# The gated sum of two branches, turned by transposing transfers in place of TensorE, in a decoder block on one Trainium2 core

## The chip, the cores and the metric

One NeuronCore of one Trainium2 chip runs the kernel. It has five engines that run beside each other, each with its own queue of instructions: TensorE (PE, matmuls; its weight loads are listed as PEld), VectorE (DVE), ScalarE (ACT), GpSimd (POOL) and SyncE (SP), which in this kernel mostly issues DMAs. The metric is the device time of one execution in microseconds (us); lower is better.

## What is computed

A decoder block over 256 positions of width 2048, in float32. The part that matters here:

```python
proj = a @ w_in[layer]                       # a = rmsnorm(h, ...)
q_a, k_a, v_a, q_r, f_r, i_r, g_r, gate_a, gate_r = split_columns(proj)
...
y = jax.nn.sigmoid(gate_a) * (attn @ w_attn_branch[layer]) + jax.nn.sigmoid(gate_r) * (r_out @ w_hgrn_branch[layer])
h = h + rmsnorm(y @ w_mix_out[layer], norm_mix_post[layer])
a = rmsnorm(h, norm_ffn_pre[layer])
gt, up = jnp.split(a @ w_ffn_gate_up[layer], [D_FF], axis=-1)
ff = (jax.nn.silu(gt) * up) @ w_ffn_down[layer]
h = h + rmsnorm(ff, norm_ffn_post[layer])
```

`attn` is a dilated sliding-window attention, `r_out` a gated linear recurrence; `y` is 256 x 2048, `w_mix_out` 2048 x 2048. To multiply `y` by `w_mix_out`, the contracted dimension, y's columns, must lie on the 128 partitions: y has to be transposed in between.

## The kernel before

**Matmuls.** Every weight and every activation is split into a high part (fp32r, ScalarE) and a low part (what is missing, VectorE), and a product is three matmuls: high by high, high by low, low by high. Weights come in by DMA into one of three `raw` slots, are split into one of three `w` slots, and are read by TensorE. A loop at the end of `tile_hybrid_block` goes over a list of items. For item i it first calls `prepare(i)`, which splits the weights of item i+2 and issues the load that is three `raw` slots further on, then issues the matmuls of item i, and then resumes, one step each, the generators that hold the rest of the work: `evacs` (reading out finished accumulators), `turned`, `turns` (two resumptions per item, L1663), and the `lanes`. A generator does the work up to its next `yield` and is resumed later; a deque of them is worked from the front, and `flush` runs it to the end. The order in which instructions are issued here is the order on each engine.

**Two kinds of items stand around the change.** The branches' weights are multiplied in blocks of 512 columns ("N" blocks), four chunks each, 12 matmuls of 128 x 512 per chunk. The four blocks of `w_attn_branch` are called B0 to B3 here, and B2c1 is chunk 1 of block B2. Two chunks share one `raw` slot. Then come the two wide blocks of `w_mix_out`, of eight steps each; the steps of the first are called s0 to s7. Six of them, (m, 0) in `MIX[0]`, have 24 matmuls and read slot m of `yT`; s3 and s6, (0, 1) and (1, 1), are done with seven products for eight, 21 matmuls, and read sums of slots 0 and 1 (`y7`, made by `pair_sums` in a lane). By the list the slots are read in this order: s0 reads slot 2, s1 slot 3, s2 slot 4, s3 slot 0, s4 slot 5, s5 slot 6, s6 slot 1, s7 slot 7.

**Accumulators.** There are four banks `acc` and four `aux`. A block B takes two of `acc`, a step s0 takes the banks (0, 0) and (0, 1) for the first half of its matmuls and (1, 0), (1, 1) for the second; the last two are those of B3, free once `evac_attn_branch(3)` has read them (L1174).

**The gated sum.** `evac_attn_branch(j)` is resumed in the three items after block j's last chunk. The first two multiply the accumulators by the gate and add the other branch's part (L1174, L1175), so that y_j, 256 x 512, lies in the gate's own tile; the third appends the generator `turned` of y_j to `turns`. Here that is called round j; it makes slots 2j and 2j+1 of `yT`. For each slot it issues four transposes of 128 x 128 on TensorE into an `aux` bank (L598), yields, then calls `put`: high part on ScalarE (L575), low part on VectorE (L579), and yields. What a step reads comes through `after(turns)`: where the slot isn't there yet, the generators in `turns` are resumed on the spot until it is, so that the step's own matmuls are issued behind them.

Before the first mix step `begin_mix` runs `evacs` to the end, loads an activation table and issues six DMAs from ScalarE's queue (L1186 to L1196). After step s1 `turns` is flushed (L1602).

**The feed-forward part** turns its own activations in another way, in `turn_act` (L1366): ScalarE splits the 32-bit words into a plane of low and a plane of high 16-bit halves (L1370), SP issues four transposing transfers of 16-bit elements (L1376), and ScalarE joins the two planes again (L1385).

Of the kernel before, what the change touches and what calls it, by code (L numbers as in the profile page):

```python
# [14 lines left out]
F32 = mybir.dt.float32  # L15
F32R = mybir.dt.float32r
I32 = mybir.dt.int32
U16 = mybir.dt.uint16
AF = mybir.ActivationFunctionType
OP = mybir.AluOpType  # L20

P = 128
S = 256
# [78 lines left out]
def tile_hybrid_block(ctx: ExitStack, tc: tile.TileContext, t, out):  # L102
    nc = tc.nc
# [12 lines left out]
    def nm(s):  # L116
        serial[0] += 1
        return f"{s}_{serial[0]}"
# [7 lines left out]
    def aux():  # L126
        return auxp.tile([P, 512], F32, tag="aux", name=nm("aux"))
# [4 lines left out]
    def p3(s, dtype, n, bufs, tag=None):  # L132
        return wide_pool[-1].tile([P, n], dtype, tag=tag or s, bufs=bufs, name=nm(s))
# [33 lines left out]
    ident = cpool.tile([P, P], F32, name="ident")  # L167
# [50 lines left out]
    blocks, chunks, wides, steps = [], [], [], []  # L218
# [27 lines left out]
    def add_wide_block(*args, **kw):  # L246
        b = Wide(*args, **kw)
        wides.append(b)
        for i in range(len(b.order)):
            n = len(steps)  # L250
            slots.append(lambda n=n: load_wide(n))
            items.append((steps, n, len(slots) - 1))
            steps.append([b, i, None, None])
# [296 lines left out]
            yield  # L550


    class Split:


# [31 lines left out]
                return self(k)  # L587
            return x

        def turned(self, src, n0, n):  # L590

            for i in range(n):
                ps = aux()
                for kk in range(2):
                    for b in range(2):
                        at = kk * S + b * P
                        c = (2 * i + kk) * P
                        nc.tensor.transpose(ps[:, at : at + P], src[:, b, c : c + P], ident)  # L598
                yield
                self.put(n0 + i, ps.rearrange("p (k t) -> p k t", k=2))  # L600
                yield

    def transpose_in(src, gcol, dst, c, apart=False):
# [43 lines left out]

    evacs, turns, lanes, queue = deque(), deque(), [deque(), deque()], deque()
    back, turned, hold = deque(), deque(), [False]
    ready = set()  # L650

    def advance(q):
        if q:
            try:
                next(q[0])
            except StopIteration:
                q.popleft()
                return

    def flush(q):  # L660
        while q:
            advance(q)
# [494 lines left out]
    yT = []  # L1157
# [10 lines left out]
    def evac_attn_branch(j):  # L1168
        def go(banks):
            if not yT:  # L1170
                yT.append(Split("yT", KD))
            y = gates["a", j]
            for i in range(2):
                nc.vector.tensor_mul(y[:, i, :], banks[i], y[:, i, :])  # L1174
                nc.vector.tensor_add(y[:, i, :], y[:, i, :], part[j][:, i, :])  # L1175
                yield
            turns.append(yT[0].turned(y, 2 * j, 2))
        return go


# [396 lines left out]
    for half in range(2):  # L1577
        for g in range(3):
            c = 1024 * g + 512 * half
# [16 lines left out]
    for j in range(2):  # L1596
        last_mix = len(wides)
        add_wide_block(t["w_mix_out"][0], (1024 * j, 1024 * j + 512), MIX[j],
                       lambda k: yT[0].after(turns)(k), lambda m: y7[m], evac_mix, j == 0,
                       pre=begin_mix if j == 0 else None)  # L1600
        if j == 0:
            wides[-1].post = lambda c: flush(turns) if c == 1 else None  # L1602
    together = len(items) - 2
    w = t["w_ffn_gate_up"][0]
    spare = None
# [28 lines left out]
    for i in range(len(items)):  # L1634
        kind, n, _ = items[i]
        b, c = kind[n][:2]
# [22 lines left out]
        if wide and c == b.turn:  # L1659
            flush(evacs)  # L1660
            turned.append(turn_act(turns.popleft()))
        advance(turned)
        for _ in range(2):  # L1663
            if turns and type(turns[0]) is not tuple:
# [71 lines left out]
```

## Time and profile before

| | |
|---|---|
| median of 3 runs | 1688.17 us (1687.39 to 1688.42) |
| the profiled execution | 1689.89 us |
| its span, first to last instruction | 1688.1 us |
| granted TensorE clock, mean | 0.999 |
| DMA, mean | 248 GB/s |
| ScalarE, busy | 983.1 us, 1102 instructions |
| VectorE, busy | 1416.6 us, 1623 instructions |

The profile is of one execution. Its times count from the span's start: the attention branch's blocks B1 to B3 and the steps s0 to s5 lie between 865 and 938 us. In a timeline a row gives start, duration, engine, line of the kernel, operation, `out<-in` by the kernel's names, the shape and the count of instructions that were merged; in brackets stands how long the engine was idle before and what ended it. `PEld`, `SPq` and `ACTq` are the weight loads and the queues of SyncE and ScalarE. Rows of one source line give the smallest, median and largest duration in ns, and then the start of the first and the last one.

### The profile page before, as it was taken

The page shows a single profiled execution, that of the slowest core. Times are in us where ns is not written, and L with a number is a line of the kernel's source. Part 1 is how long each engine was busy: PE and PEld are TensorE (multiplying, and loading weights), DVE is VectorE, ACT ScalarE, POOL GpSimd, SP SyncE. Part 2 cuts the span into 40 slices and gives each one's busy share as a digit, 9 for nine tenths or more (in the row PEclk, how much of TensorE's full clock was granted, in tenths as well). Part 3 has the DMA queues.
Part 4 walks back from the last instruction along what each step waited for, and adds up shares of the span by engine and source line. Part 5 has one row for each costly group of instructions (what it writes and reads, how often), then busy time and mean ns, then how long its engine had stood idle before and what let it go on. Part 6 is the DMA issues. An engine that isn't in the chain of part 4 may idle for free.

```text
span 1688.1 us, 21672 instructions
## 1 busy us (share of the span) xinstructions
PE 1674.2 (99%) x8169; PEld 1406.0 (83%) x8169; DVE 1416.6 (84%) x1623; ACT 983.1 (58%) x1102; POOL 3.9 (0%) x13
## 2 busy tenths in 40 slices
PE   9999999999999999999999999999999999999997
PEld 7888888888888888888888888888888888888886
DVE  6899888867987987776668888898888988898987
ACT  6655555544455545555535547676667666675653
POOL 0000000000000000000000000000000000000000
PEclk9999999999999999999999999999999999999999
DMA  8566666668777866787858556898888888887673
GB/s 278 207 232 242 224 226 227 234 231 298 233 251 250 281 226 225 254 307 264 309 175 274 194 183 209 272 282 270 272 266 283 271 274 266 277 280 267 236 256 128
DMA packets 252841, 419.26 MB, mean 248 GB/s; under 512 B 36752, under 2 KB 103488, under 8 KB 250176
## 3 DMA queue, kind: packets, MB, share of 16 engines
q1 hardware_dynamic: 242480, 379.70, 68.1%
q10 hardware_dynamic: 10192, 38.15, 5.9%
q8 instruction: 64, 1.05, 0.3%
q14 instruction: 41, 0.34, 0.1%
q0 software_dynamic: 64, 0.02, 0.0%
HBM read 376.92 MB, written 35.13 MB: 244 GB/s over the span
## 4 chain that ended last, share of the span: by engine, by line
PE 95%; DVE 2%; ACT 1%; DMA 1%; issue 1%; SPq 0%; DVEq 0%; ACTq 0%
PE acc L139 62%; PE aux L139 32%; DVE wl L421 1%; PE aux L944 0%; DMA raw<-in_w_ffn_gate_up 0%; ACT w L419 0%; DMA x<-in_x 0%; PE aux L611 0%; DVE fz L1509 0%; DVE dl L431 0%; ACT junk L1463 0%; PE aux L598 0%; DVE e L1459 0%; DVE wl L428 0%; DVE f L543 0%
## 5 line engine op out<-in xcount | busy, mean ns | idle before, releaser
L139 PE MATMUL acc<-xT,w 128*128 128x256 f32 (+1 forms) x2048 | 365.1, 338 | 0.0
L421 DVE TENSOR_TENSOR wl<-raw,w 128x2048 fp32r<-128x2048 f32 (+1 forms) x140 | 304.5, 2182 | 67.3 <-ACT w L419 65.3
L139 PEld LDWEIGHTS acc<-xT,w 128*128 128x128 f32 x2048 | 311.9, 188 | 44.7
L366 DVE TENSOR_TENSOR w<-raw,w 128x1024 fp32r<-128x1024 f32 x176 | 215.0, 1222 | 118.9 <-ACT w L365 118.3
L419 ACT ACTIVATE w<-raw 128x2048 fp32r<-128x2048 f32 (+1 forms) x140 | 254.5, 1826 | 97.4 <-PE acc L139 31.6
L365 ACT ACTIVATE w<-raw 128x1024 fp32r<-128x1024 f32 x176 | 185.9, 1058 | 192.8 <-PE acc L139 137.4
L139 PE MATMUL acc<-w,xT 128*128 128x512 f32 x578 | 168.8, 391 | 0.0
L440 ACT ACTIVATE w<-sum 128x1024 fp32r<-128x1024 f32 x57 | 60.6, 1062 | 168.5 <-DVE sum L435 161.7
L139 PE MATMUL acc<-w,hT 128*128 128x512 f32 x472 | 152.7, 391 | 0.4 <-DVE hT L1259 0.4
L448 DVE TENSOR_TENSOR wl<-sum,w 128x1024 fp32r<-128x1024 f32 x114 | 137.2, 1221 | 7.7 <-ACT w L440 7.6
L139 PEld LDWEIGHTS acc<-w,xT 128*128 128x128 f32 x578 | 108.2, 188 | 22.3
L139 PE MATMUL aux<-w,hT 128*128 128x512 f32 x374 | 120.0, 389 | 0.0
L139 PE MATMUL aux<-w,xT 128*128 128x512 f32 x344 | 109.8, 389 | 0.0
L450 DVE TENSOR_TENSOR dl<-raw,dh 128x1536 fp32r<-128x1536 f32 x57 | 100.1, 1757 | 11.3 <-ACT dh L446 8.2
L139 PEld LDWEIGHTS acc<-w,hT 128*128 128x128 f32 x472 | 88.5, 188 | 19.0 <-DVE hT L1259 0.9
L139 PE MATMUL acc<-wl,hT 128*128 128x512 f32 x236 | 91.8, 389 | 0.0
L446 ACT ACTIVATE dh<-raw 128x1536 fp32r<-128x1536 f32 x57 | 84.1, 1475 | 5.3 <-PE acc L139 3.1
L139 PE MATMUL acc<-w,a 128*128 128x512 f32 x268 | 83.7, 389 | 0.2 <-DVE e L1413 0.2
L139 PEld LDWEIGHTS aux<-w,hT 128*128 128x128 f32 x374 | 70.2, 188 | 14.5
L139 PE MATMUL acc<-w,so 128*128 128x512 f32 x240 | 80.4, 389 | 0.0
L139 PE MATMUL aux<-w,a 128*128 128x512 f32 x254 | 79.5, 389 | 0.0
L139 PEld LDWEIGHTS aux<-w,xT 128*128 128x128 f32 x344 | 64.6, 188 | 13.4
(295 smaller groups left out, 2990.2 us busy)
## 6 DMA issues: line engine op xcount, KB each, us to landing
raw<-in_w_in SPq DMA_DIRECT2D x270, 512.0 KB, 4.7
raw<-in_w_ffn_gate_up SPq DMA_DIRECT2D x156, 512.0 KB, 5.0
raw<-in_w_ffn_down SPq DMA_DIRECT2D x88, 512.0 KB, 5.4
pre<-in_w_ffn_gate_up SPq DMA_DIRECT2D x40, 512.0 KB, 6.5
presum<-pre ACTq DMA_DIRECT2D x20, 1024.0 KB, 4.7
s<-presum SPq DMA_DIRECT2D x40, 512.0 KB, 6.9
raw<-in_w_mix_out SPq DMA_DIRECT2D x32, 512.0 KB, 5.0
act<-acts SPq DMA_DIRECT2D x22, 512.0 KB, 6.2
```

What stands on the lines that cost most here:

```text
L139: nc.tensor.matmul(ps, lhsT, rhs, start=start, stop=stop, skip_group_check=True)
L365: nc.scalar.activation(wh, raw, AF.Copy)
L366: nc.vector.tensor_sub(wl, raw, wh.bitcast(F32))
L419: nc.scalar.activation(hi[:, c], raw[:, c], AF.Copy)
L421: nc.vector.tensor_sub(lo[:, c], raw[:, c], hi[:, c].bitcast(F32))
L440: nc.scalar.activation(hi[:, :1024], s[:, :1024], AF.Copy)
L446: nc.scalar.activation(dhi, d, AF.Copy)
L448: nc.vector.tensor_sub(lo[:, c], s[:, c], hi[:, c].bitcast(F32))
L450: nc.vector.tensor_sub(dlo, d, dhi.bitcast(F32))
```

## The change

`Split.turned` no longer uses TensorE. A round now takes a second tile `flat` of 128 x 1024 words (tag "so", four buffers) and does this:

- ScalarE splits each half of y_j into two planes of 16-bit halves in `flat` (two instructions, `halves_apart`);
- SP issues four transposing transfers of 128 x 512 16-bit elements each, from `flat` into the tile of y_j, seen as two planes;
- six yields;
- ScalarE joins both planes into 32-bit words in `flat` (one instruction, `halves_joined`), and a yield;
- `put` of the two slots as before, now from `flat`, a yield after each.

The flush of `turns` moves from after s1 to after s4.

```diff
+    def halves_apart(flat, words):
+        nc.scalar.activation(
+            flat.bitcast(U16).rearrange("p (z c) -> p z c", z=2),
+            words.bitcast(U16).rearrange("p (c z) -> p z c", z=2), AF.Copy,
+        )
+    def halves_joined(words, planes):
+        nc.scalar.activation(
+            words.bitcast(U16).rearrange("p (c z) -> p z c", z=2), planes, AF.Copy
+        )
...
-        def turned(self, src, n0, n):
-            for i in range(n):
-                ps = aux()
-                for kk in range(2):
-                    for b in range(2):
-                        at = kk * S + b * P
-                        c = (2 * i + kk) * P
-                        nc.tensor.transpose(ps[:, at : at + P], src[:, b, c : c + P], ident)
+        def turned(self, src, spent, n0):
+            for b in range(2):
+                halves_apart(spent[:, b, :], src[:, b, :])
+            planes = src.rearrange("p b c -> p (b c)").bitcast(U16).rearrange(
+                "p (z k t) -> p z k t", z=2, k=4
+            )
+            for b in range(2):
+                for z in range(2):
+                    nc.sync.dma_start_transpose(
+                        planes[:, z, :, b * P : (b + 1) * P],
+                        spent[:, b, :].bitcast(U16)[:, z * 512 : (z + 1) * 512],
+                    )
+            for _ in range(6):
                 yield
-                self.put(n0 + i, ps.rearrange("p (k t) -> p k t", k=2))
+            words = spent.rearrange("p b c -> p (b c)")
+            halves_joined(words, planes.rearrange("p z k t -> p z (k t)"))
+            yield
+            for i in range(2):
+                self.put(n0 + i, words[:, i * 512 : (i + 1) * 512].rearrange("p (k t) -> p k t", k=2))
                 yield
...
-            turns.append(yT[0].turned(y, 2 * j, 2))
+            flat = p3("flat", F32, 1024, 4, "so").rearrange("p (b c) -> p b c", b=2)
+            turns.append(yT[0].turned(y, flat, 2 * j))
...
-            wides[-1].post = lambda c: flush(turns) if c == 1 else None
+            wides[-1].post = lambda c: flush(turns) if c == 4 else None
```

## The prediction

> **What bounds the kernel now.** I read the page's first part and its chain first, then the timeline of PE around the mix.
>
> ```profile
> PE 1674.2 (99%) x8169; PEld 1406.0 (83%) x8169; DVE 1416.6 (84%) x1623; ACT 983.1 (58%) x1102; POOL 3.9 (0%) x13
> PE 95%; DVE 2%; ACT 1%; DMA 1%; issue 1%; SPq 0%; DVEq 0%; ACTq 0%
> ```
>
> PE is busy for 99% of the span and 95% of the chain that ends last runs over it. So time leaves the kernel when PE gets less to do, and comes in whenever PE waits; what ACT, DVE or the DMAs get to do is free only as long as PE does not wait for it. The timeline of PE, from chunk B3c0 to mix step s4:
>
> ```profile
> 892.14 8.46 PE L139 MATMUL acc<-w,attnT 128*128 128x512 f32 x36
> ...
> 900.43 0.60 PE L598 MATMUL aux<-ident,gate 128*128 128x128 f32 x4
> 900.79 2.99 PE L139 MATMUL acc<-w,attnT 128*128 128x512 f32 x12
> 903.62 0.60 PE L598 MATMUL aux<-ident,gate 128*128 128x128 f32 x4
> 903.97 0.48 PE L139 MATMUL acc<-w,yT 128*128 128x512 f32 x1
> ...
> 907.19 0.50 PE L139 MATMUL acc<-w,yT 128*128 128x512 f32 x1 [0.21 <-DVE gate L1174]
> ...
> 910.05 0.60 PE L598 MATMUL aux<-ident,gate 128*128 128x128 f32 x4
> 910.40 0.48 PE L139 MATMUL acc<-w,yT 128*128 128x512 f32 x1
> ...
> 915.95 0.60 PE L598 MATMUL aux<-ident,gate 128*128 128x128 f32 x4
> 916.30 0.48 PE L139 MATMUL acc<-w,yT 128*128 128x512 f32 x1
> ...
> 921.88 0.39 PE L139 MATMUL aux<-w,so 128*128 128x512 f32 x1
> ...
> 926.64 0.39 PE L139 MATMUL acc<-w,yT 128*128 128x512 f32 x1
> ```
>
> Columns are start, duration, instruction and, in brackets, idle time. From 921.88 to 926.64 are the 21 matmuls of s3: 0.227 us each, so a chunk of 12 takes 2.72 and a step of 24 takes 5.45. Four transposes hold PE from 900.43 to 900.79, 0.36 us, and the 12 matmuls behind them take 2.83 up to 903.62, 0.11 more than 2.72. A group of four costs about 0.46 us. The transposes stand where nothing waits: PE has no idle time in these rows but 0.21 us at 907.19, for an accumulator bank that DVE's gate product frees.
>
> **What the change takes away.**
>
> ```profile
> L598 PE MATMUL aux<-ident,gate x32: 270/272/273, 876.8 to 916.3; 128*128 128x128 f32 x32
> L575 ACT ACTIVATE yT<-aux x8: 577/598/600, 877.4 to 918.2; 128x512 fp32r<-128x512 f32 x8
> L579 DVE TENSOR_TENSOR yT<-aux,yT x8: 680/688/693, 878.0 to 920.1; 128x512 fp32r<-128x512 f32 x8
> L575 ACT ACTIVATE a<-act x44: 609/614/632, 1436.0 to 1660.1; 128x512 fp32r<-128x512 f32 x44
> L579 DVE TENSOR_TENSOR a<-act,a x44: 680/684/695, 1438.4 to 1664.5; 128x512 fp32r<-128x512 f32 x44
> ```
>
> 32 transposes in 8 groups at 0.46 us are 3.7 us of PE. The puts stay, and their source moves from PSUM to SBUF: 0.60 and 0.69 us from aux, 0.61 and 0.68 from SBUF in the other rows, so nothing.
>
> **What it adds.** The same four operations already run in the feed-forward part (L1370 to L1385), so they have rows:
>
> ```profile
> L1370 ACT ACTIVATE e<-e x20: 1037/1042/1060, 1089.7 to 1468.8; 128x1024 uint16<-128x1024 uint16 x20
> L1385 ACT ACTIVATE act<-e x20: 1337/1374/1385, 1101.5 to 1482.2; 128x1024 uint16<-128x1024 uint16 x20
> 1093.47 6.33 SPq L1376 DMA_TRANSPOSE e<-e  x4
> 1101.52 2.61 ACT L1385 ACTIVATE act<-e 128x1024 uint16<-128x1024 uint16 x2 [0.74 <-DMA e<-e]
> L1376 SPq DMA_TRANSPOSE e<-e x4: 1337/1890/2399, 1418.5 to 1424.1; - x4
> DMA to landing us min/median/max: 4.3/6.8/8.3
> raw<-in_w_mix_out SPq DMA_DIRECT2D x32, 512.0 KB, 5.0
> ```
>
> A round gets two splits into planes at 1.04 us (ACT), four transposing transfers, and one join. The join takes both planes at once, 2048 halves; no row shows that. A pair of 1024 each took 2.61 us (1101.52), one alone 1.37; I take 2.6; 1.4, the lower end, would take 4 x 1.2 = 4.8 us off the sum. The transfers were issued from 1093.47, and the ACT instruction that needs them all could start at 1101.52: 8.0 us. In the other window the last was issued at 1424.1 and landed 4.3 later, 9.9 us after the first issue at 1418.5. A plain 512 KB load lands in 5.0, the lower end. I take 8.0. Each round is thus a serial chain of 2.1 + 8.0 + 2.6 + 0.6 = 13.3 us ahead of the first matmul that reads it, and 0.7 more ahead of the third, which reads the low part. In before, that was 0.36 + 0.6.
>
> By the Trainium skill (Advanced Engine Details and Errata, X-Bar Transpose) a transposing DMA is as fast as a regular one. The rows here do not agree for four small ones issued one behind the other; by that rule the first rival below would hold.
>
> **Where these chains lie.** The generator is resumed twice per chunk or step. It starts the transfers in its 1st resumption, joins in the 7th, puts in the 8th and 9th and ends in the 10th, and rounds queue behind each other. y_0 is evacuated by B1c2, so round 0 has resumptions 1 and 2 after B1c2, 3 and 4 after B1c3, 5 and 6 after B2c0, joins after B2c1 and ends after B2c2. In the same way round 1 starts after B2c3, joins after B3c2; round 2 starts only after s0, and s2 itself, which reads slot 4, pulls its join; round 3 starts after s3, is flushed after s4, and s5 reads slot 6. In the trace ACT, DVE and SP keep the program's order, so I follow their queues in the trace's own times. What I need:
>
> ```profile
> 874.23 1.06 ACT L365 ACTIVATE w<-raw 128x1024 fp32r<-128x1024 f32 x1 [1.65 <-PE acc L139]
> 880.22 0.88 SPq L270 DMA_DIRECT2D raw<-in_w_attn_branch  x2
> 896.72 0.28 DVE L523 SCALAR_TENSOR_TENSOR s<-f 128x128 f32<-128x128 f32 x1
> 897.65 1.22 DVE L366 TENSOR_TENSOR w<-raw,w 128x1024 fp32r<-128x1024 f32 x1
> 903.65 2.28 DVE L421 TENSOR_TENSOR wl<-raw,w 128x2048 fp32r<-128x2048 f32 x1
> 904.25 0.60 ACT L575 ACTIVATE yT<-aux 128x512 fp32r<-128x512 f32 x1 [0.78 <-PE aux L598]
> 904.87 1.28 ACT L1186 ACT_TABLE_LOAD   x1
> 906.46 0.68 DVE L1174 TENSOR_TENSOR gate<-acc,gate 128x512 f32<-128x512 f32 x1
> 908.52 1.92 ACT L419 ACTIVATE w<-raw 128x2048 fp32r<-128x2048 f32 x1 [2.37 <-DVE gate L1174]
> 918.68 1.92 ACT L419 ACTIVATE w<-raw 128x2048 fp32r<-128x2048 f32 x1
> SPq L288 <- DMA raw<-in_w_mix_out: 8.8, 2, 7.1
> ```
>
> A chunk's high part takes 1.06 on ACT and its low part 1.22 on DVE, a mix step's 1.92 and 2.28. Each waits for the weight slot of three items before, so it starts when PE ends that item, and PE reads it two items later.
>
> *Round 0.* Splits behind the 874.23 row: 875.3 to 877.4. SP's next load waits for the low part of B2c1, now at 879.7, and ends at 880.6. Transfers 880.6 to 888.6, join 891.2, put 891.8. Behind the join on ACT stands the high part of B3c0: 892.9, low part 894.1. PE, four groups earlier, is there at 892.14 - 1.8 = 890.3. It ends B3c0 at 894.1 + 11 x 0.227 = 896.6 and not 893.0: **3.6 lost**.
>
> *Round 1.* High part of B3c1 894.6, splits 896.7; SP's load, behind the low part of B3c1, ends at 897.5; transfers until 905.5, join 908.1, put of slot 2 908.7, low 909.4. PE is through B3c3 at 904.8 and waits for slot 2 until 908.7: 3.9. Behind the put: high part of s1 910.6, its low part on DVE 912.9, low of slot 3 913.6, the four small sums 1.0 (896.72 to 897.65) 914.6, and only then the gate product (0.68) that frees the bank of s0's second half, 915.3, where before it ended at 907.14. The first half ends at 909.4 + 10 x 0.227 = 911.7, so PE waits another 3.6. s0 ends at 918.0; before at 910.05: **8.0 behind**, all transposes so far credited.
>
> *Round 2.* ACT behind the last put (911.2): table load and six DMA issues, 904.85 to 908.52 before, so 914.9; high part of s2 916.8; splits 918.9. SP: the load of s5 waits for the first half of s4's load to land (7.1 us of SP waiting in the last row; 8.1 from that load's issue behind the low part of s1), 921.1, ends 922.0. Transfers until 930.0, join 932.6, put of slot 4 933.2, low 933.9. s1 ends at 918.0 + 5.5 = 923.5: PE waits 9.7. s2 ends at 933.9 + 22 x 0.227 = 938.9; before 921.88: **17.0 behind**.
>
> *Round 3.* High part of s5 waits for the end of s2: 941.0; splits 943.1; low part 943.3, SP's load 944.2, transfers 952.2, join 954.8, put 955.4, low 956.1. s4 ends at 938.9 + 4.8 + 5.4 = 949.1: PE waits 6.3. s5 ends at 956.1 + 5.0 = 961.1; before at 926.64 + 2 x 5.45 = 937.5: **23.6 behind**. Nothing gives that back, since PE is the bound of what follows. The rest of the added ACT work (19 us in all) and the loads that stand behind transfers on SP cost nothing: ACT is idle 42% of the span, and the tightest load, that of s4, lands at 921.0 for a split at 923.5. Without that cover a late load would hold PE by its lateness.
>
> **The clock.** PE has no gap like these in before except at the ends:
>
> ```profile
> 1.19 3.31 PE L139 MATMUL aux<-warm 128*128 128x512 bf16 x8 [1.19 <-DVE warm L163]
> 1678.18 0.39 PE L139 MATMUL aux<-w,a 128*128 128x512 f32 x1
> 1680.00:1688.10 8.10, 0.00 (x0) 0.00 (x0) 3.55 (x9) 0.65 (x4) 0.00 (x0) 0.71 0.39 129
> ```
>
> After the last matmul (1678.57) the granted clock averages 0.71 from 1680.0: a fall to half at about 1683.4, 4.8 us after PE stopped. The first eight matmuls took 3.31 us, 1.5 more than 8 x 0.227. So I price each gap over 4.8 us, those of 9.7 and 6.3, at 1.5 us: 3.0. Bounds: 0 and, with the gaps of s0, 6.
>
> By the Trainium skill (TensorE: Matmul & The Clock Gate, Part 1) an idle window of about 3.4 us halves the clock and 3.4 us of work restores it; by that, as an estimate, one of the gaps of s0 could cost 1.7 as well.
>
> **Sum.** 23.6 + 3.0 = 26.6 us, with the 3.7 saved in it. The profiled execution took 1689.9 (span 1688.1); with the change 1716.5. The median of the runs is 1.7 lower: 1688.2 + 26.6 = **1714.8 us**.
>
> **Rivals.**
> *The transfers cost what a plain load costs.* With 5.0 for 8.0 every chain is 3.0 shorter, and the four add up where each round starts later for the one before: 23.6 - 12 = 11.6, and one gap (6.7 at s2) still trips the clock: 13.1, **1701.3 us**. For it: the 5.0 row. Against: the four are issued one by one, some 1.3 to 2.4 us each, and both windows above took longer. This is what the Trainium skill's rule on X-Bar Transpose would give.
> *Not slower: all is hidden.* Then 3.7 of PE and the 0.2 at 907.19 go: **1684.3 us**. Its place is s2. Between the end of the high part of s2 (910.44) and the end of s1 (916.30) there are 5.9 us in before; the splits, join and put take 5.3 of them. It holds if the four transfers land within 0.6 us, or if round 2 starts a block earlier than I count.
> *Worse.* With 9.9 for 8.0 four chains give 7.6 more and a third gap trips the clock: 23.6 + 7.6 + 4.5 = 35.7, **1723.9 us**. For it: the second window took that long. Against: the first took 8.0.
> *The change does not do what it says* (TensorE keeps its transposes): 1688.2.
>
> **How the numbers follow.** Forecast 0.68, plain-load price 0.15, worse 0.09, hidden 0.05, no change 0.03. The range reaches from the first rival to the worse one: 1701 to 1724; below it lie the last two, 0.08, and some of each end. A measurement of this kernel tells 0.2%, 3.4 us, from no change. Faster 0.05, same 0.03, slower 0.92.
>
> **What would show it.** In the profile after: no L598 on PE; ACT's joins waiting for transposing transfers, four times, the longest in s1 to s2; PE idle ahead of B3c0, twice in s0 (ended by a put of yT, then by the gate product), about 10 us ahead of s2 and 6 ahead of s5; a granted clock under 1.00 behind these two; the same pace everywhere else. I am wrong if the joins start without waiting, if PE's wait at s2 is short, or if the stretch from B1c2 to s5 is under 10 us longer.

## The result and the profile after

| | before | after |
|---|---|---|
| median of 4 runs each | 1687.88 us (1687.39 to 1688.42) | 1713.53 us (1711.58 to 1713.74) |
| the profiled execution | 1689.89 us | 1713.74 us |
| its span | 1688.1 us | 1711.8 us |
| granted TensorE clock, mean | 0.999 | 0.992 |

The ratio is 1.0148 [1.0135, 1.0160]: the changed kernel is about 25 us slower, 23.7 us between the two profiled spans. The predicted time was 1714.8 us, with a range of 1701 to 1724. That is close, but two errors of opposite sign lie under it, and what its rivals said of a quicker landing was wrong.

The first part of the page and the first line of the chain, of after:

```profile
PE 1679.1 (98%) x8137; PEld 1407.5 (82%) x8137; DVE 1416.9 (83%) x1623; ACT 1000.4 (58%) x1114; POOL 3.8 (0%) x13
PE 88%; DVE 4%; DMA 3%; ACT 2%; issue 1%; SPq 1%; ACTq 0%; DVEq 0%
```

PE has 32 instructions fewer (8169 to 8137) and yet more busy time (1674.2 to 1679.1): some matmuls ran slower. ACT has 12 instructions and 17.3 us more. The chain lost 7% of PE to waits on DVE, DMA and ACT. The timeline of PE in after shows which:

```profile
889.85 0.50 PE L139 MATMUL acc<-w,attnT 128*128 128x512 f32 x1 [0.91 <-ACT w L365]
891.11 10.99 PE L139 MATMUL acc<-w,attnT 128*128 128x512 f32 x47 [0.76 <-DVE w L366]
904.74 0.50 PE L139 MATMUL acc<-w,yT 128*128 128x512 f32 x1 [2.64 <-ACT yT L588]
...
911.00 0.79 PE L139 MATMUL acc<-w,yT 128*128 128x512 f32 x1 [2.94 <-DVE gate L1196]
...
914.02 0.39 PE L139 MATMUL acc<-wl,yT 128*128 128x512 f32 x1
...
920.39 0.39 PE L139 MATMUL acc<-w,yT 128*128 128x512 f32 x1
929.13 0.80 PE L139 MATMUL acc<-w,yT 128*128 128x512 f32 x1 [8.35 <-ACT yT L588]
...
934.61 0.39 PE L139 MATMUL acc<-wl,yT 128*128 128x512 f32 x1
...
952.56 0.79 PE L139 MATMUL acc<-w,yT 128*128 128x512 f32 x1 [5.07 <-ACT yT L588]
...
958.25 0.39 PE L139 MATMUL acc<-wl,yT 128*128 128x512 f32 x1
...
960.76 0.39 PE L139 MATMUL acc<-dh,yT 128*128 128x512 f32 x1
```

The idle times in brackets stand at the places that the prediction named: ahead of B3c0 (0.91 and 0.76), in s0 (2.64 for the put of slot 2, 2.94 for the gate product), ahead of s2 (8.35) and of s5 (5.07). They add up to 20.7 us. No transpose stands on PE any more. The bracket-free rows bound three slow stretches: from 911.00 to 914.02 are 7 matmuls, from 929.13 to 934.61 are 13, from 952.56 to 958.25 are 13. At 0.227 us each they would take 1.59, 2.95 and 2.95; they took 3.02, 5.48 and 5.69, so 1.4, 2.5 and 2.7 us more, 6.7 in all. The clock granted in three windows of after (from:to, length, busy time of PE, PEld, DVE, ACT and POOL, PEclk, DMA share, GB/s) says why:

```profile
910.00:914.00 4.00, 3.00 (x7) 2.40 (x8) 3.93 (x7) 3.67 (x4) 0.00 (x0) 0.57 1.04 400
924.00:934.00 10.00, 4.87 (x12) 3.81 (x13) 2.39 (x3) 3.63 (x3) 0.00 (x0) 0.50 0.76 224
951.00:958.00 7.00, 5.44 (x13) 4.24 (x14) 3.59 (x3) 3.79 (x4) 0.00 (x0) 0.53 0.29 109
```

The account closes: 20.7 us of waits and 6.7 of slow clock, less 3.7 for the transposes and less the 0.2 us wait of before at 907.19, are 23.5. The first row of s6 in the timeline of PE, of before:

```profile
937.52 0.39 PE L139 MATMUL acc<-dh,yT 128*128 128x512 f32 x1
```

In after s6 starts at 960.76, 23.2 us later. Behind it nothing is given back: the spans differ by 23.7.

The queues of ScalarE and SyncE in after, from round 0's transfers to round 3's join:

```profile
885.66 2.52 ACT L562 ACTIVATE flat<-gate 128x2048 uint16<-128x2048 uint16 x1 [3.78 <-DMA gate<-flat]
...
901.54 2.49 ACT L562 ACTIVATE flat<-gate 128x2048 uint16<-128x2048 uint16 x1 [2.87 <-DMA gate<-flat]
...
912.67 1.99 ACT L555 ACTIVATE flat<-gate 128x1024 uint16<-128x1024 uint16 x2
917.04 1.06 ACT L440 ACTIVATE w<-sum 128x1024 fp32r<-128x1024 f32 x1 [2.38 <-DVE sum L435]
...
920.87 1.91 ACT L419 ACTIVATE w<-raw 128x2048 fp32r<-128x2048 f32 x1
925.93 2.48 ACT L562 ACTIVATE flat<-gate 128x2048 uint16<-128x2048 uint16 x1 [3.15 <-DMA gate<-flat]
...
949.36 2.48 ACT L562 ACTIVATE flat<-gate 128x2048 uint16<-128x2048 uint16 x1 [2.74 <-DMA gate<-flat]
```

```profile
878.77 5.22 SPq L612 DMA_TRANSPOSE gate<-flat  x4
...
894.40 5.15 SPq L612 DMA_TRANSPOSE gate<-flat  x4
...
916.67 6.47 SPq L612 DMA_TRANSPOSE gate<-flat  x4
...
942.57 5.18 SPq L612 DMA_TRANSPOSE gate<-flat  x4
```

From the first issue of a round to the start of its join are 6.9, 7.1, 9.3 and 6.8 us. Four times a join waits for transfers (2.7 to 3.8 us), and at s2 too the landing is what comes last. But look at what stands ahead of round 2's join: the splits of the weights of s3 (from 917.04) and of s4 (920.87). ScalarE comes free of them only at 922.8, 2.0 us after s1 ended on PE, and join and put (2.5 + 0.6 us) were still to come. That is what the experiments turn on.

### The profile page after: what moved, and what is told of

Same layout as the page of the kernel before. It is cut to its first block, busy times and chain, and to the rows that moved or that the text cites. A ratio compares the mean times of both kernels' runs of the same rounds, so it can differ in the third digit from the quotient of the medians.

```text
span 1711.8 us, 21644 instructions
## 1 busy us (share of the span) xinstructions
PE 1679.1 (98%) x8137; PEld 1407.5 (82%) x8137; DVE 1416.9 (83%) x1623; ACT 1000.4 (58%) x1114; POOL 3.8 (0%) x13
## 4 chain that ended last, share of the span: by engine, by line
PE 88%; DVE 4%; DMA 3%; ACT 2%; issue 1%; SPq 1%; ACTq 0%; DVEq 0%
PE acc L139 57%; PE aux L139 31%; DVE wl L421 1%; DMA raw<-in_w_ffn_gate_up 1%; DMA gate<-flat 1%; ACT w L419 1%; SPq L612 1%; ACT flat L562 1%; DMA raw<-in_w_ffn_down 1%; PE aux L966 0%; DVE sum L435 0%; DMA e<-e 0%; DVE dl L450 0%; DVE wl L448 0%; PE aux L633 0%
```

## The experiments

Two theories. **Landing**: what costs is the time that the transfers take; a quicker landing would give nearly all of it back. **Place**: what costs is where join and put stand in ScalarE's queue, behind weight splits that themselves wait for PE; the transfers could land at once and most of the cost would stay. Beside both, the clock: how much is lost to matmuls at half speed. The times of before on the same chips had medians of 1688.82 (the first four experiments), 1689.24 (the next four) and 1689.09 us (the last three).

### PE's gaps filled with matmuls of zeros

13 matmuls of zeros are put in the middle of s0, 38 ahead of s2 and 24 ahead of s5, into the accumulator (0, 0) of the block, which is open there and stays as it is.

```diff
+            if b is wides[last_mix - 1] and c == 0:
+                fill(b, 13)
...
+        if b is wides[last_mix - 1] and c in (2, 5):
+            fill(b, {2: 38, 5: 24}[c])
...
+    def fill(b, n):
+        for _ in range(n):
+            mm(b.bank[0, 0], warm[:, :P], warm, False, False)
```

> The changed kernel, with matmuls of zeros by zeros added to an open accumulator where TensorE has nothing to do: 13 in the middle of s0, 38 ahead of s2, 24 ahead of s5. They take no longer than the waits that stand there. Theory of the clock (after each of these waits the matmuls run at half clock, 0.2 us more each, 7 of them in s0, 12 in s2, 13 in s5; what s0 loses is taken up by the wait at s2): 5.0 us less than the changed kernel, about 1708.5. Rival (the slow matmuls are only the price of waiting, or the fillers themselves push the step back): 1713 or more.

Measured: 1711.11 us, 1.0136 [1.0121, 1.0151]. PE's timeline and a window of the run with the gaps filled:

```profile
919.76 8.38 PE L139 MATMUL acc<-warm 128*128 128x512 bf16 x37
930.53 0.50 PE L139 MATMUL acc<-w,yT 128*128 128x512 f32 x1 [2.40 <-ACT yT L596]
...
959.40 0.39 PE L139 MATMUL acc<-dh,yT 128*128 128x512 f32 x1
```

```profile
931.00:935.00 4.00, 4.00 (x11) 2.93 (x10) 0.80 (x2) 0.00 (x1) 0.00 (x0) 0.57 0.27 98
951.00:958.00 7.00, 6.99 (x30) 4.37 (x29) 3.44 (x3) 4.79 (x4) 0.00 (x0) 1.00 0.43 139
```

Where the zeros reached up to the step (s5), the clock stayed at 1.00; at s2 they ended too early, and a gap of 2.40 us brought one fall. From s2's first matmul to s6's are 28.87 us (930.53 to 959.40), in after 31.63 (929.13 to 960.76): 2.8 us less. But s2 itself started 1.4 us later, and the interval of the total overlaps that of after. The total lies between the two expectations, 1708.5 and 1713, and decides neither. So the slow clock is real and can be held off; its size is shown by the matmuls' own spacing, and by the total it stays unclear.

### No transfers at all

The four transfers of each round are left out, and the join puts the split halves back where they came from; the slots then hold y untransposed, so the product with `w_mix_out` is another one. Splits, join, puts, waits on ScalarE and the order stay.

```diff
-            for b in range(2):
-                for z in range(2):
-                    nc.sync.dma_start_transpose(
...
-            halves_joined(words, planes.rearrange("p z k t -> p z (k t)"))
+            words = src.rearrange("p b c -> p (b c)")
+            nc.scalar.activation(
+                words.bitcast(U16).rearrange("p (b c z) -> p z b c", b=2, z=2),
+                spent.rearrange("p b c -> p (b c)").bitcast(U16).rearrange("p (b z c) -> p z b c", b=2, z=2),
+                AF.Copy,
+            )
```

> The changed kernel without its 16 transposing transfers; the planes are split and joined as before, six yields lie between, and the slots get y as it is, not transposed. Theory of the serial chain (the join waits for the transfers, and what waits behind the join is PE): the wait of 8.4 us at s2 shrinks to the 5 us or so of high part of s4, join and put that still stand ahead of slot 4 on ScalarE, s5 waits some 2.5 us, the losses in B3c0 and s0 vanish: 9 us over before, 10 with the clock, about 1697.5. Rival (ScalarE's extra 19 us is what costs): it stays near 1713. Rival (the transfers' place in SP's queue costs, not the waiting): under 1690.

Measured: 1703.9 us, 1.0093 [1.0076, 1.0110]. Some 15.7 of the 25 us (by the interval 12.8 to 18.6) remain without a single transfer, far more than the 9 to 10 expected. PE's and ScalarE's timelines of this run:

```profile
905.59 0.50 PE L139 MATMUL acc<-w,yT 128*128 128x512 f32 x1 [2.94 <-DVE gate L1194]
...
915.27 0.39 PE L139 MATMUL acc<-w,yT 128*128 128x512 f32 x1
923.54 0.80 PE L139 MATMUL acc<-w,yT 128*128 128x512 f32 x1 [7.88 <-ACT yT L588]
...
943.14 0.50 PE L139 MATMUL acc<-w,yT 128*128 128x512 f32 x1 [2.23 <-ACT yT L588]
```

```profile
914.82 1.06 ACT L440 ACTIVATE w<-sum 128x1024 fp32r<-128x1024 f32 x1 [1.74 <-DVE sum L435]
...
918.55 1.89 ACT L419 ACTIVATE w<-raw 128x2048 fp32r<-128x2048 f32 x1
920.35 2.48 ACT L613 ACTIVATE gate<-flat 128x2048 uint16<-128x2048 uint16 x1
922.86 1.15 ACT L588 ACTIVATE yT<-gate 128x512 fp32r<-128x512 f32 x2
```

The wait ahead of s2 is 7.88 us, hardly less than the 8.35 of after, and from 909 us on nothing on ScalarE waits for a DMA: it is in the middle of the splits of s3 and s4 when PE ends s1 at 915.5, and the join has its turn at 920.35. This floor is in the program. The loop issues `prepare(s2)`, the split of s4's weights, before s2 resumes the generator that joins slot 4. That split reuses the weight tile of s1, so it cannot begin before PE ends s1. Behind it come the join and the put: 1.9 + 2.5 + 0.6 = 5.0 us of PE waiting at s2 at the least, whatever a transfer costs. The two waits that only landing made, ahead of B3c0 and for slot 2, are gone here.

### Two rounds by transfers, two by TensorE

```diff
+            if j not in (0, 1):
+                turns.append(yT[0].turned_pe(y, 2 * j, 2))
+                return
```

`turned_pe` is the generator of before. The second run has (2, 3) in place of (0, 1). The flush stands after s1 in the first run, after s4 in the second.

> Rounds 0 and 1 by transfers, rounds 2 and 3 by TensorE, flush after s1 as before. By the waits of the changed kernel: 1.7 in B3c0, 2.8 and 3.1 in s0, 1.4 of clock, less 1.8 of TensorE saved: 6.7 to 7.2 us over before, about 1695. If the loss came from the traffic in the saturated steps s0 to s2 alone, under 1689.

> Rounds 0 and 1 by TensorE, rounds 2 and 3 by transfers. By the queues: round 2 can start no earlier than after s0, s2 waits about 8 us and s5 about 5.5, less 1.8 saved: 12.8, with 2.5 us of slow clock behind each of the two waits 17.8: 1700.5 to 1705.7. The two halves should add up to the whole, 24 to 25.7, if each round's loss is its own; well under, if one round's lateness hides the other's.

Measured: 1696.8 us, 1.0048 [1.0033, 1.0063] with rounds 0 and 1; 1709.31 us, 1.0126 [1.0111, 1.0141] with rounds 2 and 3. The first fits; the second is above what was expected, and the two together are 8.1 + 21.3 = 29.4 us, more than the 25 of all four. ScalarE and PE of the run with rounds 2 and 3:

```profile
910.58 2.59 ACTq L1235 DMA_DIRECT2D hx<-in_x  x4
913.29 1.91 ACT L419 ACTIVATE w<-raw 128x2048 fp32r<-128x2048 f32 x1 [9.19 <-DMA gate<-flat]
```

```profile
925.67 0.80 PE L139 MATMUL acc<-w,yT 128*128 128x512 f32 x1 [11.40 <-ACT yT L588]
```

With rounds 0 and 1 out of the queue, round 2 starts before `begin_mix` and not after s0. Then a weight split waits 9.19 us, and the profile puts the end of its wait down to transfers that it does not read. Ahead of it on ScalarE stand only the table load and the DMA issues of `hx`. The next experiments look at that.

### Before, with the transfers beside it, read by nobody

To the kernel before are added the 16 transfers of after, from y into a tile that nothing reads. In the first run they are issued at the start of each round; in the second those of rounds 2 and 3 come at the end of their rounds, so behind the DMAs of `begin_mix`. The diff is that of the second, against before:

```diff
+            if n0 < 4:
+                self.transfers(src, spent)
             for i in range(n):
                 ps = aux()
...
+            if n0 >= 4:
+                self.transfers(src, spent)
```

> The kernel before, with the 16 transposing transfers issued where each round starts, from y into a tile that nobody reads. Theory of the place (what costs is that PE's data stand behind join and weight splits on ScalarE and behind the landing; the traffic itself is hidden): 0 to 1.5 us over before. Rival (the transfers hold up SP's loads in the stretch where the DMA queues are full): 5 us or more.

> The kernel before with 16 transfers that nobody reads, as in the run of that kind before it (8.3 us over), but those of round 2 issued after s0 and those of round 3 after s1, behind the six DMAs that ScalarE's queue issues ahead of s0. Theory of the shared landing (those six DMAs wait for the landing of round 2's transfers, 12 us in which ScalarE holds back the high part of s2): the wait at s2 goes, 0 to 2 us over before, under 1691.5. Rival (the moved bytes slow the weight loads): 5 us or more over before wherever the transfers stand.

Measured: 1697.55 us, 1.0051 [1.0036, 1.0066], and 1689.31 us, 0.9998 [0.9989, 1.0008]. ScalarE and PE of the first:

```profile
910.81 6.10 ACTq L1205 DMA_DIRECT2D hx<-in_x  x4
917.03 1.91 ACT L419 ACTIVATE w<-raw 128x2048 fp32r<-128x2048 f32 x1 [12.07 <-DMA flat<-gate]
```

```profile
918.99 0.80 PE L139 MATMUL acc<-w,yT 128*128 128x512 f32 x1 [3.55 <-ACT w L419]
921.32 0.80 PE L139 MATMUL acc<-wl,yT 128*128 128x512 f32 x1 [1.53 <-DVE wl L421]
```

ScalarE of the second:

```profile
908.01 1.92 ACT L419 ACTIVATE w<-raw 128x2048 fp32r<-128x2048 f32 x1 [2.91 <-DMA raw<-in_w_mix_out]
```

There the split waits 2.91 us. The same 16 transfers cost some 8 us in the one place (5.1 of them these two waits of PE, and behind them half clock: the matmuls from 922 on stand 0.43 apart) and nothing that could be told in the other. So moving the data is free there. What costs is DMA issues on ScalarE that stand still until transfers issued shortly before, on another queue and to other data, have landed, with the split of s2's weights behind them: it waits 12.07 us, where in before it waited 2.37.

The traces show why. A DMA counts up a semaphore when it lands. All DMAs of SyncE's and ScalarE's queues share eight of these semaphores in this program, and a DMA is not issued until the one that had its semaphore before it has landed: of the 851 such pairs in the first run none breaks this. In the first run three of the four `hx` issues share with transposing transfers of round 2:

| `hx` issue | the DMA that had its semaphore before | issued | landed | `hx` issued |
|---|---|---|---|---|
| 1 | transposing transfer | 902.30 | 910.79 | 910.81 |
| 2 | `gpost` | 903.07 | 910.75 | 911.24 |
| 3 | transposing transfer | 903.54 | 912.87 | 912.94 |
| 4 | transposing transfer | 905.22 | 916.51 | 916.53 |

In the second run, as in before, all four share with plain weight loads; the last of these landed at 907.57, the last issue went out at 907.59, and the split began at 908.01. In the run with rounds 2 and 3 above, the first `hx` issue stood for a plain weight load too (landed 910.56, issued 910.58), and the other three for transposing transfers that landed at 911.04, 911.54 and 912.01.

### The rounds side by side

In after a round waits in the deque until the round ahead of it has ended. Here every round in it is resumed twice per item; in the second run the number of yields between transfers and join is also fitted to each round (the last two lines of the diff).

```diff
-        for _ in range(2):
-            if turns and type(turns[0]) is not tuple:
-                advance(turns)
+        for x in list(turns):
+            if type(x) is tuple:
+                break
+            for _ in range(2):
+                if next(x, turns) is turns:
+                    turns.remove(x)
+                    break
...
-            for _ in range(6):
+            for _ in range((10, 8, 4, 6)[n0 // 2]):
```

> The changed kernel, but each generator in the queue is resumed twice per item, not the first one alone, so that round 2 starts after B3c2 and joins after s1, and round 3 starts after s0 and joins after s3. Theory of the place: the waits at s2 and s5, 8.4 and 5.1, and the slow clock behind them go; the losses of B3c0 and s0 stay or grow, since the splits of round 2 now stand ahead of s1's high part: by the queues 17 us over before, or less, 1700 to 1706. Rival (the transfers' traffic is the cost): no better than the changed kernel, 1713.

> As the kernel with the generators side by side, and 10, 8, 4 and 6 yields in rounds 0 to 3 in place of 6, so that each join is issued when its transfers should have landed and not behind the splits of s3 and s4. The same instructions, in another order. Theory of the place: most of the loss goes, 4 us over before by the queues (a wait for the gate product in s0 remains), 1690 to 1696. Rival (the work itself costs): 1705 or more.

Measured: 1707.12 us, 1.0106 [1.0091, 1.0121], just above what was expected, and 1695.26 us, 1.0033 [1.0022, 1.0044]. In the first PE still waits 7.80 us ahead of s2, with the join again behind the splits of s3 on ScalarE, and these behind the DMA issues of `hx`, the first of which stood until 917.04. It also waits 4.81 us at the start of s0 for a weight split behind round 1's join. All the waits of PE from B3c0 to s6 in the second:

```profile
903.08 0.51 PE L139 MATMUL acc<-w,yT 128*128 128x512 f32 x1 [2.29 <-ACT yT L588]
...
911.43 0.80 PE L139 MATMUL acc<-w,yT 128*128 128x512 f32 x1 [3.65 <-DVE gate L1196]
```

```profile
903.00:907.00 4.00, 3.92 (x10) 2.85 (x11) 0.69 (x1) 4.00 (x5) 0.00 (x0) 0.57 0.91 305
910.00:917.00 7.00, 5.57 (x13) 4.46 (x14) 3.36 (x6) 1.15 (x1) 0.00 (x0) 0.52 1.07 250
```

The same work as in after, the same 16 transfers, splits and joins, in another order: the waits at s2 and s5, 13.4 us in after, and their two clock falls are gone, and some 19 of the 25 us with them (0.33% of 1689 are 5.6 left). What stays are the two waits in s0 and half clock behind each. So neither the transfers nor the added work of ScalarE cost the 25 us by themselves.

### Round 3 alone, and rounds 0 and 3

The rounds are resumed side by side, and those that are not named go by TensorE. Round 3 alone was measured twice; the last run has (0, 3) in place of (3,), and 14 yields for round 0.

```diff
+            if j not in (3,):
+                turns.append(yT[0].turned_pe(y, 2 * j, 2))
+                return
```

> Rounds 0 to 2 by TensorE, round 3 by transfers, generators side by side: its join is issued after s3, one step ahead of its reader with 10 us from the start of the transfers. Theory of the place: nothing waits, 0.9 us of TensorE go, 0.5 of it is left: the same as before. If a round by transfers costs whatever its place: 4 us over before.

> Round 3 alone by transfers, generators side by side, a second time and in more rounds. One round's TensorE work is 0.9 us. Theory of the place: 0.5 to 1.9 us less than before, an interval that lies below 1. If the first result was chance: an interval with 1 in its middle.

> Rounds 0 and 3 by transfers, rounds 1 and 2 by TensorE, generators side by side, 14 yields in round 0 and 6 in round 3. Theory of the place: by the queues round 0 saves 0.9 us of TensorE and gives back 2.0, since the sums of slots 0 and 1 move later and then stand on VectorE ahead of the gate product in s0: 0.6 us over before, 1 to 2 over the kernel with round 3 alone. Rival (each round that is kept from waiting saves its 0.9): 1.8 under before.

Measured: round 3 alone 1687.64 us, 0.9989 [0.9980, 0.9998], and the second time 1687.7 us, 0.9990 [0.9981, 0.9999]; rounds 0 and 3 1691.38 us, 1.0014 [1.0005, 1.0023]. PE's only wait from B3c0 to s6 with round 3 alone, and the join and put on ScalarE:

```profile
906.47 0.50 PE L139 MATMUL acc<-w,yT 128*128 128x512 f32 x1 [0.20 <-DVE gate L1209]
```

```profile
924.65 2.55 ACT L562 ACTIVATE flat<-gate 128x2048 uint16<-128x2048 uint16 x1
927.24 0.63 ACT L588 ACTIVATE yT<-flat 128x512 fp32r<-128x512 f32 x1
```

The join starts without a wait, steps ahead of s5, and its put is long done when s5 needs it. So round 3 hides whole: eight transposes, two groups at 0.46 us, leave PE, and the kernel is some 1.5 us faster than before, twice, with the upper end of each interval just under 1. The transposes account for 0.9 us of that; the rest lies within the intervals. This beats both kernels, by less than the 0.2% that one measurement tells. Round 0 does not hide even with 14 yields: PE waits in the middle of s0,

```profile
907.89 0.50 PE L139 MATMUL acc<-w,yT 128*128 128x512 f32 x1 [2.67 <-DVE gate L1209]
```

for the gate product, because slots 0 and 1 come late and their small sums for s3 and s6, with the step that prepares them (1.5 us in all), now stand ahead of it on VectorE.

## Why the prediction was right, and where it was wrong

**Right: the places and the sign.** PE is the bound, so every wait of PE counts in full. All the waits that the prediction listed are there, ended by what it named, and none is there that it did not list. The late gate product (2.94 us) is one that only following the queues shows: on VectorE the low parts of s1 and of slot 3 stand ahead of it, late because their high parts stood behind the join, and then the four small sums, which take 0.9 of the 2.94. One sign did not come as named: the longest wait of a join was round 0's (3.78 us), not that between s1 and s2 (3.15). The join at 2.48 us (2.6 predicted), the splits at 1.0 each and the puts at no cost were as priced, and the second run of transfers read by nobody showed that the traffic itself can be free.

**Mis-sized: the waits.** They came to 20.7 us where the prediction's add up to 27.1.

| | predicted | measured |
|---|---|---|
| ahead of B3c0 | 3.6 | 1.7 |
| s0, slot 2 | 3.9 | 2.6 |
| s0, gate product | 3.6 | 2.9 |
| ahead of s2 | 9.7 | 8.35 |
| ahead of s5 | 6.3 | 5.1 |
| slow clock | 3.0 | 6.7 |

The term was the 8.0 us from first issue to join, taken from the feed-forward part; it was 6.9, 7.1 and 6.8 in three rounds. Round 2's was longer, 9.3, but SP began it 5.3 us earlier than predicted (916.67 for 922.0).

**Wrong step: "I price each gap over 4.8 us".** The threshold was read from the end of the run, where nothing follows the gap. The clock fell already in s0, with gaps of 2.64 and 2.94 us, and in two other runs after single gaps of 2.29 (at 903.08) and 2.40 (at 930.53). And a fall cost up to 2.7 us, not 1.5, where PE was back before the clock was. By the Trainium skill (TensorE: Matmul & The Clock Gate, Part 1) 3.4 us of work restore the clock, and for the idle window it gives about the same 3.4 us. A window of 4 us with a mean of 0.57 holds 4 x 0.43 / 0.5 = 3.4 us at half speed, and the windows at 910, 931 and 903 us all show that; but behind the long gaps it took more, 5.5 and 5.7 us of work in s2 and s5. And the gaps of s0 were shorter than 3.4 us, and the second brought the clock down all the same.

The times at which the granted clock changes explain both. In after it falls at 910.44, 924.09 and 951.40 and rises at 913.85, 934.33 and 958.23. These lie 1, 3, 3, 5 and 2 times 3.413 us apart, and in every other run all changes of the clock, from the first to the last, lie a whole number of 3.413 us apart too. So the clock is set anew at fixed times, one every 3.41 us, by what PE did since the last of them. Between 860 and 990 us, where it falls in after and in eight other runs, it fell each time that PE had stood idle for 1.9 us or more of the 3.41, and not where it had for 1.5 or less; it rose again only after a stretch with less than 0.6 us idle (matmuls of zeros count as work). The gap of 2.64 us in after lay across such a time (903.61) and brought no fall; that of 2.29 us lay within one stretch and did. The 4.8 us at the end of before are the rest of one stretch and the whole of the next. Where these times lie differs between the profiles (the first rise of the clock is at 4.09 us in before, at 5.91 in after and at 6.53 in the run with filled gaps), so 6.7 us is what this one execution lost.

The prediction gave the rule's estimate for s0 (1.7 for one gap; 1.4 measured) beside its sum and went by its own reading of the rows, which was the worse of the two. This error (3.7 us too little) and the waits (6.4 too much) offset each other to 2.7, near the 2.9 between the 26.6 predicted and the 23.7 measured between the spans. That the forecast came within 1.3 us of the measured median is to that extent luck.

**Wrong step: what would hold PE at s2 if the transfers were quick.** The prediction made the landing of round 2's transfers the end of the chain. In after it was: the join waited 3.15 us for it. But two rivals hang on there being nothing close behind it: 1701.3 us if the transfers cost what a plain load costs, and all hidden, 1684.3, "if the four transfers land within 0.6 us". Without any transfers the kernel takes 1703.9, by the interval some 1701 to 1707. So quicker transfers could not have brought 1684.3, and 1701.3 lies at the edge of what the kernel takes with none at all: the count of 5.9 us between the high part of s2 and the end of s1 left out that the splits of s3 and s4 lie ahead of the join in ScalarE's queue, and that s4's waits for PE. Of the 25 us some 9.3 go with the transfers, and some 15.7 stay, which are place: the join behind weight splits, the late gate product, and the half clock behind these waits. The two overlap at s2, where PE waited 8.35 us with transfers and 7.88 without. The rounds side by side with fitted yields show it from the other end, with the same transfers and 5.6 us over before.

**Not foreseen:** that rival's other condition, "or if round 2 starts a block earlier than I count", does not suffice either. Where round 2 started before `begin_mix` and s2 pulled its join, the DMA issues of `hx` held ScalarE up (the split behind them waited 9.19 us) and s2 waited 11.40 us, more than in after. Only with fitted yields did s2 not wait, and there PE had lost 5.9 us in s0 already.

## What to carry to other kernels

Moving work off the bounding engine pays only if its replacement can stand in the helper's in-order queue ahead of anything that waits for the bounding engine itself; so list what is issued between the source being ready and the consumer, not only the durations. A join pulled by its consumer stands behind the prefetch of the steps after it, and no faster transfer mends that; an earlier place does. Change one round at a time: here rounds 0 and 1 hid in no order that was run, round 2 only behind the delay that they made, and round 3 whole, for two groups of transposes.

## What the runs showed of the hardware that was not expected

- A DMA issue waited for the landing of another DMA with no data in common, even of another queue: in this program the DMAs of both queues share eight completion semaphores, and an issue stands until the last DMA of its semaphore has landed. In the kernel before with unread transfers, `hx` issues on ScalarE's queue went out 0.02 to 0.07 us after the landing of SyncE's transposing transfers of the same semaphore, and the weight split behind them waited 12.07 us. With the transfers issued behind them the split waited 2.91. Plain loads do the same: in before the last `hx` issue went out at 908.10, 0.02 us after a weight load had landed.
- Four transposing transfers of 128 KB take 5.2 to 6.5 us of SyncE's queue to issue in after, some 1.3 us or more each, so the last one starts when more than half of the round's time is over. The join could start 1.6 to 2.8 us behind the end of the last issue.
- The granted clock changes only at times 3.413 us apart. It halves where PE has stood idle for 1.9 us or more since the last such time, and did not for 1.5, so a gap of 2.29 us halved it and one of 2.64, which lay across such a time, did not. One fall in after cost 1.4 to 2.7 us of work behind it. Matmuls of zeros that reach up to the step keep it at 1.00.
